# Six of eleven gate/up pairs of a feed-forward layer formed with seven block products in place of eight

## The chip, the cores and the metric

The kernel runs on one core of a Trainium2 chip. Its engines work side by side, each through its own queue in program order: TensorE (PE; PEld are its weight loads), VectorE (DVE), ScalarE (ACT), GpSimd (POOL) and SyncE (SP), which issues most of the transfers. The metric is the device time of one execution in microseconds (us).

## The reference, cut to what matters

One decoder layer over 256 tokens of width 2048, all in 32-bit floats: RMSNorm, two token mixers (gated linear attention and dilated attention) merged by gates, then the feed-forward part, which the change touches:

```
hf = _rmsnorm(x, ffn_norm[l])
gu = hf @ w_ffn_in[l]                       # 256 x 2048 times 2048 x 11264
gate, up = gu[..., :D_FF], gu[..., D_FF:]   # D_FF = 5632
x = x + (jax.nn.silu(gate) * up) @ w_ffn_out[l]
out = _rmsnorm(x, final_norm)
```

## The kernel before, in words

Every large product is a `Job`: a weight matrix's 512 columns, all of its rows, and two groups of 128 tokens (a "T" job). A job goes through its rows in k tiles of 128. One transfer (a unit, `raw`, three buffers) brings four k tiles of 512 columns, and a unit is worked off in two subs of two k tiles each. `split` writes a sub's weights as a rounded part `wh` (ScalarE, L121) and the rest `wl = raw - wh` (VectorE, L184), 1024 elements in each partition; there are `LA + 1 = 5` buffers of each. `mains` then issues three matmuls with 512 columns for each k tile and token group, hi·wh, hi·wl and lo·wh, where hi and lo are the two parts of the transposed activations: 12 matmuls in a sub, 96 in a job of 16 k tiles.

The order is written out by hand in the main loop at the end of the kernel. At each sub it calls `next_split` (the split of the sub four places on, and after a unit's last one the next transfer), then the evacuation of the job that has just ended (`pending.evac`), then a hook of the job, then `advance`, `mains` and `advance` again. `advance` takes a step of a queue of small tasks, such as `turn_block`, which transposes a finished block on TensorE into `psa` and splits it into hi and lo. So on ScalarE and VectorE the split of the sub four places on stands ahead of the evacuation of the job that has ended, and its `wh` buffer is the one that this job's last sub reads.

The feed-forward part has eleven pairs. `pair(p)` is a gate job (its evacuation is a Silu on ScalarE into `sg`) and an up job (its evacuation is two scalar_tensor_tensor on VectorE, L794, which multiply and push `turn_block`). After pairs 4 and 8, and at the end, `down` adds four jobs of `w_ffn_out`, over four, four and three pairs. PSUM has eight banks: `acc` is four, handed out in turn, `psa` is two and `psb` two. `fpair` takes the banks of successive jobs in turn, two `acc`, two `psb`, two `acc`, so that a job begins in banks that the job ahead of it did not use. The last job is issued by code of its own behind the loop.

## Time and profile before

| | |
|---|---|
| median of 3 runs | 1886.39 us (1885.41 to 1886.59) |
| the profiled execution's own time | 1885.85 us |
| its span, first to last instruction | 1884.1 us |
| TensorE busy | 1869.7 us, 99% of the span |
| VectorE busy | 1025.3 us, 54% |
| ScalarE busy | 861.5 us, 46% |
| granted TensorE clock, mean | 0.998 |

The profile gives each engine's busy time, the chain of work that ended last, and, for any stretch, the instructions in order with what ended the idle time before each. A matmul's row shows 0.39 us, but successive matmuls overlap, so the pace is read from the distance of their starts. An idle time of an engine other than TensorE costs nothing here as long as TensorE goes on.

### The profile page before, as it was taken

The page shows a single profiled execution, that of the slowest core. Times are in us where ns is not written, and L with a number is a line of the kernel's source. Part 1 is how long each engine was busy: PE and PEld are TensorE (multiplying, and loading weights), DVE is VectorE, ACT ScalarE, POOL GpSimd, SP SyncE. Part 2 cuts the span into 40 slices and gives each one's busy share as a digit, 9 for nine tenths or more (in the row PEclk, how much of TensorE's full clock was granted, in tenths as well). Part 3 has the DMA queues.
Part 4 walks back from the last instruction along what each step waited for, and adds up shares of the span by engine and source line. Part 5 has one row for each costly group of instructions (what it writes and reads, how often), then busy time and mean ns, then how long its engine had stood idle before and what let it go on. Part 6 is the DMA issues. An engine that isn't in the chain of part 4 may idle for free.

```text
span 1884.1 us, 22852 instructions
## 1 busy us (share of the span) xinstructions
PE 1869.7 (99%) x9324; PEld 1587.7 (84%) x9324; DVE 1025.3 (54%) x1146; ACT 861.5 (46%) x1071; POOL 22.3 (1%) x35
## 2 busy tenths in 40 slices
PE   8999999999999999999999999999999999999998
PEld 8988988888888888888888888888888888888886
DVE  6446646745665466555554555444455454454454
ACT  6446545544454454544444455444443444434443
POOL 0000000000000000000000000000000000000001
PEclk9999999999999999999999999999999999999999
DMA  7554455456555565465657655555555555555553
GB/s 251 205 198 158 167 189 165 162 184 195 174 174 179 200 193 172 161 218 199 207 190 243 231 179 195 186 199 180 198 181 200 193 187 184 196 189 191 196 182 114
DMA packets 207297, 356.31 MB, mean 189 GB/s; under 512 B 6123, under 2 KB 66599, under 8 KB 207192
## 3 DMA queue, kind: packets, MB, share of 16 engines
q1 hardware_dynamic: 202192, 346.18, 54.2%
q0 software_dynamic: 1728, 5.51, 1.3%
q10 hardware_dynamic: 3272, 3.16, 0.6%
q8 instruction: 73, 1.20, 0.3%
q14 instruction: 32, 0.26, 0.0%
HBM read 352.70 MB, written 2.13 MB: 188 GB/s over the span
## 4 chain that ended last, share of the span: by engine, by line
PE 98%; DVE 1%; ACT 0%; DMA 0%; issue 0%; SPq 0%; DVEq 0%; ACTq 0%
PE acc L234 67%; PE psb L234 12%; PE acc L216 9%; PE acc L218 5%; PE psa L696 1%; PE psa L550 0%; PE psb L595 0%; PE psa L471 0%; PE psb L453 0%; PE psb L560 0%; PE psb L597 0%; PE psa L571 0%; DMA o<-in_x_dram 0%; PE psa L301 0%; PE psa L234 0%; PE psb L398 0%
## 5 line engine op out<-in xcount | busy, mean ns | idle before, releaser
L184 DVE TENSOR_TENSOR wl<-raw,wh 128x1024 fp32r<-128x1024 f32 (+2 forms) x655 | 794.5, 1216 | 794.2 <-ACT wh L121 791.9
L121 ACT ACTIVATE wh<-raw 128x1024 fp32r<-128x1024 f32 (+2 forms) x655 | 685.5, 1049 | 874.2 <-PE acc L234 639.9
L234 PE MATMUL acc<-wh,h 128*128 128x512 f32 (+2 forms) x2496 | 768.5, 386 | 0.0
L234 PEld LDWEIGHTS acc<-wh,h 128*128 128x128 f32 x2496 | 467.2, 188 | 91.4 <-issue 2.0
L234 PE MATMUL acc<-wl,h 128*128 128x512 f32 (+2 forms) x1248 | 479.9, 385 | 0.0
L216 PE MATMUL acc<-h,wh 128*128 128x512 f32 x768 | 274.4, 401 | 0.0
L234 PEld LDWEIGHTS acc<-wl,h 128*128 128x128 f32 x1248 | 235.0, 188 | 44.2
L218 PE MATMUL acc<-h,wl 128*128 128x256 f32 x768 | 214.5, 279 | 0.0
L234 PE MATMUL acc<-wh,z 128*128 128x512 f32 (+1 forms) x648 | 199.2, 386 | 0.0
L216 PEld LDWEIGHTS acc<-h,wh 128*128 128x128 f32 x768 | 144.2, 188 | 34.4 <-ACT wh L121 0.7
L218 PEld LDWEIGHTS acc<-h,wl 128*128 128x128 f32 x768 | 144.8, 189 | 0.4
L234 PEld LDWEIGHTS acc<-wh,z 128*128 128x128 f32 x648 | 121.1, 188 | 24.3
L234 PE MATMUL acc<-wl,z 128*128 128x512 f32 (+1 forms) x324 | 125.0, 386 | 0.0
L234 PE MATMUL psb<-wh,h 128*128 128x512 f32 x384 | 119.9, 390 | 0.0
L234 PE MATMUL psb<-wh,z 128*128 128x512 f32 x304 | 94.9, 390 | 0.0
L234 PE MATMUL acc<-h,wh 128*128 128x256 f32 x512 | 92.5, 283 | 0.0
L234 PEld LDWEIGHTS psb<-wh,h 128*128 128x128 f32 x384 | 72.1, 188 | 14.9
L234 PEld LDWEIGHTS acc<-h,wh 128*128 128x128 f32 x512 | 80.0, 192 | 0.2
L234 PE MATMUL acc<-wh,o 128*128 128x512 f32 x256 | 79.5, 389 | 0.0
L234 PE MATMUL psb<-wl,h 128*128 128x512 f32 x192 | 74.7, 389 | 0.0
L234 PE MATMUL acc<-h,wl 128*128 128x256 f32 x256 | 72.4, 283 | 0.0
L234 PEld LDWEIGHTS acc<-wl,z 128*128 128x128 f32 x324 | 60.9, 188 | 12.1
(202 smaller groups left out, 1151.9 us busy)
## 6 DMA issues: line engine op xcount, KB each, us to landing
raw<-in_w_in_dram SPq DMA_DIRECT2D x144, 1024.0 KB, 4.7
raw<-in_w_ffn_in_dram SPq DMA_DIRECT2D x88, 1024.0 KB, 4.8
raw<-in_w_ffn_out_dram SPq DMA_DIRECT2D x44, 1024.0 KB, 5.0
raw<-in_w_branch_gla_dram SPq DMA_DIRECT2D x16, 1024.0 KB, 5.0
raw<-in_w_out_dram SPq DMA_DIRECT2D x16, 1024.0 KB, 5.0
...
```

What stands on the lines that cost most here:

```text
L121: nc.scalar.activation(o, i, func, **kw)
L184: nc.vector.tensor_sub(wl[:, :k * n], src, wh[:, :k * n].bitcast(F32))
L216: nc.tensor.matmul(job.acc[j], wh[:, kk, j * P:(j + 1) * P], hl.both(aj), start=first, stop=last, skip_group_check=True)
L218: nc.tensor.matmul(job.acc[j][:, 0:S], wl[:, kk, j * P:(j + 1) * P], hi, start=False, stop=last, skip_group_check=True)
L234: nc.tensor.matmul(dst, st, mv, start=first and i == 0 and j % per_bank == 0, stop=last and i == 2, skip_group_check=True)
L696: nc.tensor.transpose(pt[:, j * S + a * P:j * S + a * P + P], src[:, a, j * P:(j + 1) * P], ident)
```

## The change

Pairs 1, 3, 4, 6, 8 and 10 become one job of kind "S" each, which forms gate and up together. A unit of it is one step: two k tiles, with the 512 columns of gate and the 512 of up, brought by two transfers. In steps 0, 1, 2, 4, 5 and 6 of eight (`FAST`) the block product of two token groups by two k tiles with two k tiles by gate and up is formed by Strassen's algorithm in Winograd's form: seven block products in place of eight, so 21 matmuls in place of 24. They take sums of weight blocks (`sums`, three subtractions on VectorE into `t`) and sums of activation blocks (`x1_forms`, made once after the norm, six steps). Steps 3 and 7 keep eight products. A fast step has four subs with 3, 6, 6 and 6 matmuls (`b11`, `b2`, `t13`, `t24`); a plain step two with 12.

The products of a job stand in all eight PSUM banks; `evac_step1` and `evac_step2` add them up into gate and up. The other five pairs stay two "T" jobs, but now always with `acc` for gate and `psb` for up. `turn_up` holds the transposition of a T pair that stands ahead of an S job until the S job has ended. `down` now follows pairs 3 and 7, and `fpair` counts the down jobs alone. `final_norm` is loaded at the last `down`.

```diff
+            if st in job.fast:
+                plan = (("b11", ((0, "a11", "p1"),)), ("b2", ((0, "a12", "p2"), (1, "s4", "p3"))),
+                        ("t13", ((0, "s1", "p5"), (1, "s3", "p7"))), ("t24", ((0, "s2", "p6"), (1, "a22", "p4"))))
...
+    def sums(sub):
...
+        if sub["src"] == "t13":
+            t = sub["unit"]["t"] = env["fp"].tile([P, 4, 512], F32, name="t", tag="t")
+            nc.vector.tensor_sub(t[:, 0:2], b[:, :, 1], b[:, 0])
+        else:
+            t = sub["unit"]["t"]
+            nc.vector.tensor_sub(t[:, 2], b[:, 1, 1], t[:, 0])
+            nc.vector.tensor_sub(t[:, 3], b[:, 1, 0], t[:, 2])
...
+    def step_mains(sub):
...
+            acc = [ps_acc() for _ in range(4)] + ps_pair(2) + ps_pair(3)
+            job.bank = dict(zip(("p1", "p2", "p3", "p5", "p7", "p6", "p4", "p8"), acc))
...
+            act(wh, src, AF.Copy)
+            nc.vector.tensor_sub(wl, src, wh.bitcast(F32))
...
+    FAST = (0, 1, 2, 4, 5, 6)
...
+    def x1_forms():
...
+            nc.vector.tensor_add(a, t[:, :, 0].bitcast(F32), t[:, :, 1].bitcast(F32))
+            nc.vector.tensor_add(f[:, 0], a[:, 0, P:], a[:, 1, P:])
+            nc.vector.tensor_sub(f[:, 2], a[:, 0, 0:P], a[:, 0, P:])
+            nc.vector.tensor_sub(f[:, 1], f[:, 0], a[:, 0, 0:P])
+            nc.vector.tensor_sub(f[:, 3], a[:, 1, 0:P], f[:, 1])
...
+            act(b[:, 0], f, AF.Copy)
+            nc.vector.tensor_sub(b[:, 1], f, b[:, 0].bitcast(F32))
...
+    def evac_step1(job):
...
+        act(u[0], b["p1"], AF.Copy)
+        nc.vector.tensor_add(u[1], u[0], b["p6"])
+        nc.vector.tensor_add(u[2], u[1], b["p7"])
+        nc.vector.tensor_add(u[1], u[1], b["p5"])
+        nc.vector.tensor_add(u[3], u[2], b["p5"])
...
+    def evac_step2(p):
...
+            nc.vector.tensor_add(z[:, 0], u[0], b["p2"])
+            act(z[:, 0], z[:, 0], AF.Silu, scale=env["rstd2"][:, 0:1])
...
-    def pair(p):
-        for col, ev in ((512 * p, evac_fgate(p)), (FF + 512 * p, evac_fup(p))):
+    def pair(p, hold):
+        for col, ev in ((512 * p, evac_fgate(p)), (FF + 512 * p, evac_fup(p, hold))):
...
-                    {5: lambda: drain("X")} if first else None, pairs=fpair()))
+                    {5: lambda: drain("X")} if first else None, pairs=[3] if col >= FF else [0]))
+
+    def fast_pair(p):
+        def start():
+            drain("F")
+            drain("A")
+            drain("A2")
...
+        job.pre[len(job.subs) - 2] = lambda: evac_step1(job)
...
-            pre = {2 * (n - 1): lambda: drain("A")} if c == 0 else None
+            pre = {2 * (n - 2): lambda: drain("A"), 2 * (n - 1): lambda: drain("A2")} if c == 0 else None
...
+    fastp = (1, 3, 4, 6, 8, 10)
     for p in range(11):
-        pair(p)
-        if p == 4:
-            down(0, 4, False)
-        if p == 8:
-            down(4, 4, False)
+        if p in fastp:
+            fast_pair(p)
+        else:
+            pair(p, p + 1 in fastp and p != 7)
+        if p in (3, 7):
+            down(p - 3, 4, False)
...
+            if i + 1 < len(subs):
+                sums(subs[i + 1])
             split(subs[i])
```

On VectorE, the end of the up job of pair 1 and the first subs behind it before (`wl` is a split's second half, `raw` the weights as they were loaded, `sg` the pair's block in evacuation):

```order
L184 TENSOR_TENSOR wl_9800<-raw_9696,wh_9799 128x1024 [waits Activation_49]
L184 TENSOR_TENSOR wl_9818<-raw_9735,wh_9817 128x1024 [waits DMAHW5_49,Activation_49]
L184 TENSOR_TENSOR wl_9834<-raw_9735,wh_9833 128x1024 [waits Activation_49]
L184 TENSOR_TENSOR wl_9852<-raw_9769,wh_9851 128x1024 [waits DMAHW6_49,Activation_49]
L794 SCALAR_TENSOR_TENSOR sg_9714<-acc_9717,r_ffn_9306,sg_9714 128x512
L794 SCALAR_TENSOR_TENSOR sg_9714<-acc_9718,r_ffn_9306,sg_9714 128x512 [waits PE_49]
L184 TENSOR_TENSOR wl_9874<-raw_9769,wh_9873 128x1024 [waits Activation_49]
```

and one fast step of the first S job now (`t` holds the sums of weight blocks):

```order
L275 TENSOR_TENSOR wl_9737<-raw_9663,wh_9736 128x512 [waits DMAHW4_49,Activation_49]
L194 TENSOR_TENSOR t_9746<-raw_9663 128x1024 [waits DMAHW5_49,DVE_49]
L275 TENSOR_TENSOR wl_9749<-raw_9663,wh_9748 128x1024 [waits Activation_49]
L197 TENSOR_TENSOR t_9746<-raw_9663,t_9746 128x512 [waits DVE_49]
L198 TENSOR_TENSOR t_9746<-raw_9663,t_9746 128x512 [waits DVE_49]
L275 TENSOR_TENSOR wl_9761<-t_9746,wh_9760 128x1024 [waits Activation_49]
L275 TENSOR_TENSOR wl_9777<-t_9746,wh_9776 128x1024 [waits Activation_49]
```

For the weights of two k tiles with gate and up, VectorE had two instructions over 1024 elements and has seven, four over 1024 and three over 512.

On TensorE, the first six matmuls of a gate job before (its two banks are the two `acc`):

```order
L234 MATMUL acc_12195<-wh_12119,h0_8791 128x512 [waits Activation_49]
L234 MATMUL acc_12195<-wl_12120,h0_8791 128x512 [waits DVE_49]
L234 MATMUL acc_12195<-wh_12119,h0_8791 128x512
L234 MATMUL acc_12196<-wh_12119,h0_8791 128x512
L234 MATMUL acc_12196<-wl_12120,h0_8791 128x512
L234 MATMUL acc_12196<-wh_12119,h0_8791 128x512
```

and of the gate job behind the first S job now (`acc_9980` and `acc_9981` are the banks that held the products p1 and p2):

```order
L339 MATMUL acc_9980<-wh_9900,h0_8787 128x512 [waits Activation_49]
L339 MATMUL acc_9980<-wl_9901,h0_8787 128x512 [waits DVE_49]
L339 MATMUL acc_9980<-wh_9900,h0_8787 128x512
L339 MATMUL acc_9981<-wh_9900,h0_8787 128x512 [waits DVE_49]
L339 MATMUL acc_9981<-wl_9901,h0_8787 128x512
L339 MATMUL acc_9981<-wh_9900,h0_8787 128x512
```

The fourth matmul has a wait on VectorE that it had not. On VectorE, what stands at that border now, from the S job's last split to the first add that reads p2 (`u` and `sg` are what the products are added into):

```order
L275 TENSOR_TENSOR wl_9889<-raw_9780,wh_9888 128x1024 [waits DMAHW3_49,Activation_49]
L286 TENSOR_TENSOR wl_9901<-raw_9830,wh_9900 128x1024 [waits DMAHW4_49,Activation_49]
L286 TENSOR_TENSOR wl_9911<-raw_9830,wh_9910 128x1024 [waits Activation_49]
L286 TENSOR_TENSOR wl_9923<-raw_9873,wh_9922 128x1024 [waits DMAHW5_49,Activation_49]
L943 TENSOR_TENSOR u1_9927<-u0_9926,psa_9629 128x512 [waits Activation_49]
L944 TENSOR_TENSOR u2_9928<-u1_9927,psa_9629 128x512 [waits DVE_49]
L945 TENSOR_TENSOR u1_9927<-u1_9927,acc_9628 128x512 [waits DVE_49]
L946 TENSOR_TENSOR u3_9929<-u2_9928,acc_9628 128x512
L286 TENSOR_TENSOR wl_9948<-raw_9873,wh_9947 128x1024 [waits Activation_49]
L286 TENSOR_TENSOR wl_9966<-raw_9892,wh_9965 128x1024 [waits DMAHW6_49,Activation_49]
L952 TENSOR_TENSOR sg_9969<-u0_9926,acc_9626 128x512
```

Five splits of the next job and four adds stand between the S job's last split and the add that frees p2's bank. The next job has the bank at once, where the job behind an evacuation had other banks before.

On VectorE in the up job of pair 0, where `x1_forms` runs now (`fa` and `ff` are its scratch, `o1` its result; before, the two `wl` followed each other):

```order
L286 TENSOR_TENSOR wl_9368<-raw_9220,wh_9367 128x1024 [waits Activation_49]
L871 TENSOR_TENSOR fa_9373<-h1_8788 128x512
L872 TENSOR_TENSOR ff_9374<-fa_9373 128x128 [waits DVE_49]
L873 TENSOR_TENSOR ff_9374<-fa_9373 128x128
L874 TENSOR_TENSOR ff_9374<-ff_9374,fa_9373 128x128 [waits DVE_49]
L875 TENSOR_TENSOR ff_9374<-fa_9373,ff_9374 128x128 [waits DVE_49]
L879 TENSOR_TENSOR o1_9380<-ff_9374,o1_9380 128x512 [waits Activation_49]
L286 TENSOR_TENSOR wl_9396<-raw_9262,wh_9395 128x1024 [waits DMAHW1_49,Activation_49]
```

Six such groups stand between successive splits, behind those of pair 0's first to sixth up sub. On ScalarE the copy that L879 waits for stands between the `wh` of the two splits.

## Rows read from the trace of the kernel before

**Rows 1.** The page: busy us, share of the span; then shares of the chain.
```profile
PE 1869.7 (99%) x9324; PEld 1587.7 (84%) x9324; DVE 1025.3 (54%) x1146; ACT 861.5 (46%) x1071; POOL 22.3 (1%) x35
...
PE 98%; DVE 1%; ACT 0%; DMA 0%; issue 0%; SPq 0%; DVEq 0%; ACTq 0%
```

**Rows 2.** Timeline of TensorE, up job of pair 0: start us, duration us, instruction, count.
```profile
1168.02 0.39 PE L234 MATMUL psb<-wh,h 128*128 128x512 f32 x1
...
1189.78 0.39 PE L234 MATMUL acc<-wh,h 128*128 128x512 f32 x1
```

**Rows 3.** Timeline of VectorE in pairs 0 and 1, idle time before in brackets.
```profile
1191.08 1.23 DVE L184 TENSOR_TENSOR wl<-raw,wh 128x1024 fp32r<-128x1024 f32 x1 [1.50 <-ACT wh L121]
1192.22 1.40 DVE L794 SCALAR_TENSOR_TENSOR sg<-psb,r_ffn,sg 128x512 f32<-128x512 f32 x2
```

**Rows 4.** Timeline of VectorE where its instructions follow each other closely.
```profile
456.69 2.36 DVE L184 TENSOR_TENSOR wl<-raw,wh 128x1024 fp32r<-128x1024 f32 x2 [0.33 <-PE psa L571]
458.97 0.75 DVE L319 TENSOR_TENSOR z<-acc,fold 128x256 f32<-128x256 f32 x2
459.75 0.69 DVE L321 TENSOR_TENSOR z<-z,R 128x512 f32<-128x512 f32 x1
460.36 0.55 DVE L577 TENSOR_TENSOR l<-psa,e 128x384 fp32r<-128x384 f32 x1
...
464.03 0.68 DVE L590 TENSOR_TENSOR vl<-z,vh 128x128 fp32r<-128x128 f32 x3
```

**Rows 5.** Groups of ScalarE and VectorE, feed-forward stretch 1151 to 1875 us: busy, mean ns.
```profile
L184 DVE TENSOR_TENSOR wl<-raw,wh 128x1024 fp32r<-128x1024 f32 x258 | 317.5, 1232 | 350.9 <-ACT wh L121 350.9
...
L121 ACT ACTIVATE wh<-raw 128x1024 fp32r<-128x1024 f32 x257 | 272.6, 1061 | 399.2 <-PE acc L234 264.8 <-PE psb L234 134.2
L121 ACT ACTIVATE z<-psa 128x512 fp32r<-128x512 f32 x22 | 11.8, 587 | 0.0
```

**Rows 6.** Timeline of all engines where up job 4 ends and a down job begins.
```profile
1367.44 0.39 PE L234 MATMUL psb<-wh,z 128*128 128x512 f32 x1
...
1367.63 1.06 ACT L121 ACTIVATE wh<-raw 128x1024 fp32r<-128x1024 f32 x1 [1.66 <-PE acc L234]
...
1368.73 1.23 DVE L184 TENSOR_TENSOR wl<-raw,wh 128x1024 fp32r<-128x1024 f32 x1 [1.50 <-ACT wh L121]
...
1369.87 1.40 DVE L794 SCALAR_TENSOR_TENSOR sg<-acc,r_ffn,sg 128x512 f32<-128x512 f32 x2
```

**Rows 7.** The same view some us later: a finished block is transposed and split.
```profile
1372.88 1.03 PE L696 MATMUL psa<-ident,sg 128*128 128x128 f32 x8
...
1373.67 0.48 PE L234 MATMUL psb<-wh,z 128*128 128x512 f32 x1
...
1374.04 1.07 ACT L121 ACTIVATE z<-psa 128x512 fp32r<-128x512 f32 x2
...
1375.31 1.28 DVE L105 TENSOR_TENSOR z<-psa,z 128x512 fp32r<-128x512 f32 x2
```

**Rows 8.** Timeline of TensorE at the kernel's start, matmuls of 348 columns.
```profile
6.65 1.08 PE L301 MATMUL psb<-ident,o 128*128 128x128 f32 x4 [1.57 <-DMA o<-in_x_dram]
...
8.46 0.49 PE L234 MATMUL acc<-wh,h 128*128 128x348 f32 x1
8.75 0.49 PE L234 MATMUL acc<-wl,h 128*128 128x348 f32 x1
...
10.78 0.40 PE L234 MATMUL acc<-wh,h 128*128 128x348 f32 x1
...
12.05 0.32 PE L234 MATMUL acc<-wl,h 128*128 128x348 f32 x1
12.21 0.48 PE L234 MATMUL acc<-wh,h 128*128 128x348 f32 x2
```

**Rows 9.** Stretches at the end: length, busy us of the engines, granted clock (PEclk), DMA.
```profile
1875.50:1878.00 2.50, 0.05 (x1) 0.00 (x0) 1.17 (x6) 0.91 (x4) 0.00 (x0) 1.00 0.00 0
1878.00:1884.00 6.00, 0.00 (x0) 0.00 (x0) 1.59 (x4) 0.72 (x1) 0.00 (x0) 0.50 0.46 175
```

More of the change, by code (lines that the diff above doesn't have):

```diff
@@ L145, in trunk_layer, with add_steps @@
     nc.vector.memset(epst, EPS)
+    def add_steps(job):
+        seen = {}
+        for st in range(job.nkt // 2):
+            unit = dict(job=job, k0=2 * st, k=2, raw=None)
+            units.append(unit)
+            if st in job.fast:
+                plan = (("b11", ((0, "a11", "p1"),)), ("b2", ((0, "a12", "p2"), (1, "s4", "p3"))),
+                        ("t13", ((0, "s1", "p5"), (1, "s3", "p7"))), ("t24", ((0, "s2", "p6"), (1, "a22", "p4"))))
+            else:
+                plan = tuple((f"b{a + 1}", ((0, f"a1{a + 1}", "p2"), (1, f"a1{a + 1}", "p3"),
+                                            (0, f"a2{a + 1}", "p4"), (1, f"a2{a + 1}", "p8"))) for a in range(2))
+            for src, prods in plan:
+                sub = dict(job=job, unit=unit, step=st, src=src, idx=len(job.subs), prods=[])
+                for f, a, b in prods:
+                    pr = dict(f=f, a=a, b=b, first=b not in seen, last=False)
+                    seen[b] = pr
+                    sub["prods"].append(pr)
+                job.subs.append(sub)
+                subs.append(sub)
+        for pr in seen.values():
+            pr["last"] = True
+        for i, s in enumerate(job.subs):
+            s["last"] = i == len(job.subs) - 1
@@ new lines, in raw_step @@
+    def raw_step(unit):
+        return unit["raw"].rearrange("p (a c n) -> p a c n", a=2, c=2)
+    def sums(sub):
+        if sub.get("src") not in ("t13", "t24"):
+            return
+        b = raw_step(sub["unit"])
+        if sub["src"] == "t13":
[5 more added lines that the diff above has]
+            nc.vector.tensor_sub(t[:, 3], b[:, 1, 0], t[:, 2])
@@ new lines, in step_src, with step_acts @@
+    def step_src(sub):
+        b = raw_step(sub["unit"])
+        src = sub["src"]
+        if src == "b11":
+            return b[:, 0, 0:1]
+        if src[0] == "b":
+            return b[:, int(src[1]) - 1]
+        return sub["unit"]["t"][:, 0:2] if src == "t13" else sub["unit"]["t"][:, 2:4]
+    def step_acts(job, st, a):
+        if a[0] == "s":
+            f = job.forms(st)
+            return [f[:, w, int(a[1]) - 1] for w in range(2)]
+        hl, j = job.acts(2 * st + int(a[2]) - 1)
+        q = slice(0, P) if a[1] == "1" else slice(P, 2 * P)
+        return hl.hi(j)[:, q], hl.lo(j)[:, q]
@@ new lines, in step_mains @@
+    def step_mains(sub):
+        job = sub["job"]
+        if not hasattr(job, "bank"):
+            acc = [ps_acc() for _ in range(4)] + ps_pair(2) + ps_pair(3)
+            job.bank = dict(zip(("p1", "p2", "p3", "p5", "p7", "p6", "p4", "p8"), acc))
+        for pr in sub["prods"]:
+            wh, wl = (t[:, pr["f"]] for t in sub["w"])
+            hi, lo = step_acts(job, sub["step"], pr["a"])
+            for i, (st, mv) in enumerate(((hi, wh), (hi, wl), (lo, wh))):
+                nc.tensor.matmul(job.bank[pr["b"]], st, mv, start=pr["first"] and i == 0,
+                                 stop=pr["last"] and i == 2, skip_group_check=True)
@@ L150, in add @@
         job.units = []
+        if job.kind == "S":
+            add_steps(job)
+            return
         u1 = 0
@@ L171, in dma @@
         r0 = job.row0 + unit["k0"] * P
+        if job.kind == "S":
+            for a in range(2):
+                w = job.w[r0 + a * P:r0 + a * P + P]
+                nc.sync.dma_start(raw_step(unit)[:, a],
+                                  bass.AP(tensor=w.tensor, offset=w.offset + job.col0,
+                                          ap=[list(w.ap[0]), [job.col1 - job.col0, 2], [1, n]]))
+            return
         nc.sync.dma_start(unit["raw"][:, :k * n].rearrange("p (a n) -> p a n", a=k),
@@ L188, in mains @@
         job = sub["job"]
+        if job.kind == "S":
+            step_mains(sub)
+            return
         n = job.ncols
@@ L763, in ffn_norm_chunk @@
             env["rstd2"] = col_rstd("ffn", tot, D)
+            push("F", x1_forms())
     def evac_out(c):
@@ L788, in evac_fgate, with turn_up, evac_fup @@
         return go
-    def evac_fup(p):
+    held = []
+    def turn_up(p, z, hold):
+        aT[p] = hl_block("z", 2 * p % 8)
+        held.append(turn_block(z, aT[p]))
+        if not hold:
+            while held:
+                push("A" if len(held) > 1 else "A2", held.pop(0))
+    def evac_fup(p, hold):
         def go(job):
```

53 lines of the change are left out of this document (46 added, 7 removed).

## The prediction

> **What bounds the kernel now.** I read the page first: TensorE is busy for 1869.7 of 1884.1 us and carries 98% of the chain of work that ended last; VectorE has 1025.3 us of work and ScalarE 861.5 [rows 1]. Then I read the pace of the part that changes. The up job of pair 0 starts at 1168.02 and the next job at 1189.78 [rows 2]: 21.76 us for 96 matmuls of 512 columns, 0.2267 us each, 2.72 us for a sub of twelve. VectorE subtracts once in each sub: 1.23 us, after 1.5 us idle until ScalarE's next `wh` [rows 3], and that `wh` waits for TensorE to give back its buffer; VectorE idles 350.9 us for it in the whole part [rows 5]. So TensorE sets the pace, and VectorE has a lead of four subs and no more, since there are five buffers.
>
> Because VectorE's work grows, its packed pace matters, not its durations. Two subtractions over 1024 elements take 2.36 us together, so the second starts 1.14 us after the first [rows 4]. A 512-element one is followed 0.61 us after its start (459.75 to 460.36); one that needs the result of the one just ahead starts 0.03 us after that one's end (458.97 + 0.75 to 459.75), so 0.72 us after its start. Three over 128 elements take 0.68 us, 0.20 apart [rows 4].
>
> **The change part by part.**
>
> *Matmuls.* 6 pairs x 6 steps x 3 products of parts = 108 fewer: 108 x 0.2267 = 24.5 us of TensorE time. A pair needs 43.5 us as two T jobs; an S job, with 6 x 21 + 2 x 24 = 174 matmuls, needs 39.4.
>
> *A fast step.* TensorE needs 21 x 0.2267 = 4.76 us. VectorE has four instructions over 1024 elements and three over 512, one of these waiting for its neighbour: 4 x 1.14 + 2 x 0.61 + 0.72 = 6.5 us. The last split needs ScalarE's copy of the last sum, 1.06 us [rows 5] plus a hand-over at each end, and finds one split of 1.14 to cover it: I add 0.1, so 6.6 us. ScalarE's own part, 3.5 x 1.06 = 3.7 us, fits. So VectorE sets the pace of the fast steps. Before, the same two k tiles had 2 x 1.14 us on VectorE against 5.44 on TensorE.
>
> *An S job.* At its start the splits of its first step are done. VectorE then has: the wait for the buffer and a 512-element `wh`, 0.65; that sub's split, 0.61; the evacuation of the job ahead, 1.32 (two instructions take 1.40, of which the next one overlaps 0.08 [rows 3]); the rest of step 1, 6.0; steps 2, 4, 5 and 6, 26.4; the two plain splits of step 3, 2.3. That is 37.3 us until the last split of step 6. TensorE then has, after about 0.2 us for the result to land, 5 matmuls of that sub (1.1 us) and the plain step 7 (5.44): 44.0 us. The plain steps give back what they can in this sum, as VectorE never waits in it. Against 43.5 us for the pair: +0.5 us, six times: **+3.0**. The saved matmuls are spent on waiting for VectorE.
>
> *The border behind an S job.* The next job gets the banks of p1 and p2. p1's is free early; p2's by the add that stands, on VectorE, behind the split of that job's fifth sub. From the last split of step 6 VectorE has two plain splits and three of the next job (5 x 1.14), the four adds of `evac_step1` (0.60 + 2 x 0.72 + 0.60), two more splits (2.3), and the add (0.69): 11.3 us. TensorE has in that time 0.2 + 1.1 + 5.44, and three matmuls into p1's bank, 0.7: 7.4 us. It stands still for 3.9 us, six times: **+23.4**. Without any lateness of VectorE the lower bound is read from a border of the kernel before: next job at 1367.44, `wh` at 1367.63, `wl` at 1368.73, evacuation from 1369.87 [rows 6], so 2.43 us plus 0.69 less 0.7, or 2.4 us. I take 3.9, since the count of instructions gives it.
>
> *Pair 7 into `down`.* The first down job behind up job 7 gets the same two `psb` banks. By the same rows its first matmul waits 2.43 + 0.74 = 3.2 us: **+3.2**. Borders of the kernel before have no such wait, as the banks alternate.
>
> *The last `down`.* Two finished blocks are now turned in its first job, each drained right ahead of the sub that reads it. In the rows of such a task, the transpositions start at 1372.88 and the next matmul could at 1373.67, but the first half-block's lo part is there only at 1375.31 + 0.68 [rows 7]; the third matmul, due at 1374.1, would wait 1.9 us. Twice: **+3.8**, between 0 (if the tasks are through earlier) and that. Before, only one block was pending, with two subs to spare.
>
> *The activation sums.* Each of the six groups stands between two splits, and both engines wait for each other: split 1.14, the five short ones 0.72 + 0.20 + 0.20 + 0.31 + 0.28 = 1.7, ScalarE's copy 0.59 [rows 5], then its next `wh` 1.06, with hand-overs 4.55 us for a sub that TensorE does in 2.72. After six, 11.0 us late. A split is done 2.5 us after the start of the sub four ahead (1367.44 to 1369.96 [rows 6]), so the lead is 10.9 - 2.5 = 8.4. TensorE waits 2.6 us, and VectorE enters the first S job 1.8 us late: **+4.4**, at least 0.
>
> *At nothing:* bytes loaded are the same, in 512 KB transfers, whose unit now lasts 6.6 us in place of 5.4; an S unit's transfer is due two steps later. The later load of `final_norm` has one down job (16 us) ahead of its use. Eleven transposed blocks stay eleven. TensorE's work of the next subs covers each; were weights late, every S step could wait, but the chain has 0% DMA [rows 1].
>
> **The sum.** +3.0 + 23.4 + 3.2 + 3.8 + 4.4 = +37.8 us on the profiled execution's 1885.85: 1923.7. The median is 0.5 us above that execution, so **1924 us**, 2.0% slower.
>
> Bounds. Low: borders at 2.4 (-9), no cost at the last `down` and the sums (-8), S jobs at 43.2 (-5): 1902. High: if VectorE's instructions did not overlap (1.23 and 0.69 us in full), a step takes 7.0 us, a job 2.1 more and a border 0.9 more, 18 us in all: 1942. The Trainium skill, "VectorE: DVE Perf Modes", section Terms, has it so: a flush after every instruction keeps the next from starting until the pipe is empty. By that the time would be 1942; the rows, where the next starts 0.08 us ahead of the end, are against it.
>
> **The rivals.**
>
> *The clock falls.* TensorE never stood still for long in this trace. At the end, its last matmul ended at about 1875.6 and the granted clock was 1.0 until 1878.0 and 0.5 (1.2 GHz) after that [rows 9], 2.5 us later. At the start, matmuls of 348 columns came 0.29 us apart, and 0.16 apart by 12.05; TensorE had worked without a break from 6.65, and the last matmul at the slow pace is that of 10.78, whose row is the first short one [rows 8]. So a border wait of 3.9 us can cost the clock, and each fall up to 4.3 us at half pace, 2.1 us: seven times, 15 us, 1939, which is inside my range. Worse if the short gaps of the fast steps (1.8 us of every 6.6, in pieces) do it: a step would need 21 x 0.45 = 9.5 us of TensorE, up to 2.9 more in 36 steps, up to 104 us: 2028. It decides by whether the clock stays at 1.0 within the S jobs. For it: the fall at the end. Against it: the gaps are short. Chance of this worse case 0.11.
> The Trainium skill has a rule for it ("TensorE: Matmul & The Clock Gate", "A second HAM failure mode: psum-queue depth-cycling"): frequent small idle times between groups of matmuls were seen to make the clock swing between its two levels. By that rule this rival would hold; no run here shows it.
>
> *VectorE does not hold TensorE up.* If the three- and four-dimensional patterns of the sums and splits ran faster than the flat rows, by a third or more, a step would need at most 4.76 us, the S jobs 39.4, and the borders only the 2.4: -24.5 + 14.7 + 3.2 + 3.8 = -2.8 us, 1883, no change. At twice the pace the split ahead of the evacuation halves too, the borders cost 1.5, and it ends at 1876, faster. The point is 4.76 us for seven instructions. For it: over the whole part VectorE has work for half of the time only (317.5 us of splits in 724 [rows 5]), so its total would fit. Against it: every two-operand row, in SBUF or PSUM, shows the same pace: from 0.61 us for 512 elements to 1.14 for 1024, 1.04 ns an element [rows 4]. Chances 0.05 (no change) and 0.03 (faster).
>
> **How the numbers follow.** The forecast's case has 0.81, the clock's worse case 0.11, the other two 0.08. The range, 1900 to 1955, takes in the low bound, the high bound and a clock that falls at borders on top of part of it; the worse case and the two on the other side lie outside. 0.2% is 3.8 us, about what a measurement of this kernel can tell from no change. Faster by more 0.03, within it 0.05, slower by more 0.92.
>
> **What would show it.** In the profile after, VectorE's idle time in the S jobs should be almost nil and a fast step should last 6.6 us, with TensorE waiting for `wl` (L275). S jobs of 44 us against 43.5 confirm the pace; 39.4 refute it. The matmul into p2's bank should wait for the add at L952 for 3.9 us in six places, the down job behind pair 7 for L933, 3.2 us. The L879 group should make TensorE wait in pair 0's up job. A granted clock of 0.5 inside S jobs would mean the first rival. I would be wrong at the root if VectorE shows long idle times inside the fast steps.

## The result, and the profile after

The changed kernel takes 1917.95 us (median of 4 runs, 1917.54 to 1918.85) against 1886.46 of the kernel before on the same chip: a ratio of 1.0169 (95% interval 1.0157 to 1.0182). It is 31.5 us slower; 1924 us had been forecast, 1900 to 1955 as the range. TensorE works 108 matmuls less, and the kernel is longer all the same. The page of the changed kernel, lines that answer to [rows 1]:

```profile
PE 1866.2 (97%) x9216; PEld 1566.6 (82%) x9216; DVE 1211.6 (63%) x1410; ACT 919.0 (48%) x1155; POOL 22.3 (1%) x35
...
PE 81%; DVE 11%; issue 3%; ACT 3%; DMA 1%; ACTq 0%; DVEq 0%; SPq 0%
```

The share of the chain is the line to read: VectorE had 1% of it and has 11%, although it is busy for 63% of the span only. The profiled execution (1917.97 us) comes to the feed-forward part at the same place as before (up job 0 starts at 1168.00 against 1168.02 in [rows 2]); TensorE's last matmul ends 32.1 us later. So all of the loss lies in the part that was changed, and the starts of the jobs on TensorE divide it. In the lines of the changed kernel L227 is a matmul of an S job and L339 one of any other job; L275 and L286 are VectorE's splits of the same two kinds, L194, L197 and L198 the sums of weight blocks; L132 is ScalarE (`wh`, a block's hi part, a Silu), L801 the transposing of a block and L116 its lo part; L933 is the evacuation of a T pair, L943 to L946 the adds of `evac_step1`, L952 to L959 `evac_step2`. An edit that adds or takes out a line above them moves these numbers by one.

| term of the prediction | forecast | measured, us |
|---|---|---|
| six S jobs, against 43.5 for a pair | +3.0 | +6.3 (44.5 to 44.6 each; the first 46.2, of which 1.6 stand in the next row) |
| activation sums | +4.4 | +4.1 (2.5 in up job 0, 1.6 in the first S job) |
| borders behind five S jobs | +19.5 | +7.3 (1.07, 0.97, 2.21, 1.02, 2.06) |
| pair 7 into `down` | +3.2 | +5.0 (3.3, and 1.7 by the clock) |
| last `down`, its border included | +7.7 | +9.5 |
| sum | +37.8 | +32.2 |

**The fast step.** TensorE in the second and third step of the first S job:

```profile
1198.86 0.50 PE L227 MATMUL acc<-wl,h 128*128 128x512 f32 x1 [0.79 <-DVE wl L275]
...
1201.32 0.49 PE L227 MATMUL acc<-wl,o 128*128 128x512 f32 x1 [0.81 <-DVE wl L275]
...
1205.49 0.50 PE L227 MATMUL acc<-wl,h 128*128 128x512 f32 x1 [0.46 <-DVE wl L275]
...
1207.95 0.50 PE L227 MATMUL acc<-wl,o 128*128 128x512 f32 x1 [0.79 <-DVE wl L275]
```

and VectorE beside it, one step from its first to its last instruction (the last row is two splits):

```profile
1202.48 0.69 DVE L275 TENSOR_TENSOR wl<-raw,wh 128x512 fp32r<-128x512 f32 x1
1203.08 1.22 DVE L194 TENSOR_TENSOR t<-raw 128x1024 f32<-128x1024 f32 x1
1204.21 1.22 DVE L275 TENSOR_TENSOR wl<-raw,wh 128x1024 fp32r<-128x1024 f32 x1
1205.35 0.69 DVE L197 TENSOR_TENSOR t<-raw,t 128x512 f32<-128x512 f32 x1
1206.07 0.69 DVE L198 TENSOR_TENSOR t<-raw,t 128x512 f32<-128x512 f32 x1
1206.68 2.51 DVE L275 TENSOR_TENSOR wl<-t,wh 128x1024 fp32r<-128x1024 f32 x2
```

The wait for the same `wl` comes back after 6.63 us (1198.86 to 1205.49, 1201.32 to 1207.95). No VectorE row here has an idle time in brackets, where the split in [rows 3] had 1.50 ahead of it. The starts follow each other by 0.60, 1.13, 1.14, 0.72 and 0.61, as in [rows 4]. The groups of 1194 to 1238 us show it in sum, as [rows 5] did for the kernel before (busy, mean ns, idle time before):

```profile
L275 DVE TENSOR_TENSOR wl<-t,wh 128x1024 fp32r<-128x1024 f32 x11 | 13.4, 1222 | 0.7 <-ACT wh L132 0.3
...
L194 DVE TENSOR_TENSOR t<-raw 128x1024 f32<-128x1024 f32 x5 | 6.1, 1219 | 0.0
...
L198 DVE TENSOR_TENSOR t<-raw,t 128x512 f32<-128x512 f32 x5 | 3.5, 692 | 0.2
```

**The border behind an S job.** VectorE and then TensorE behind the first one:

```profile
1233.83 3.49 DVE L286 TENSOR_TENSOR wl<-raw,wh 128x1024 fp32r<-128x1024 f32 x3
1237.24 0.68 DVE L943 TENSOR_TENSOR u<-u,psa 128x512 f32<-128x512 f32 x1
...
1239.28 0.68 DVE L946 TENSOR_TENSOR u<-u,acc 128x512 f32<-128x512 f32 x1
1239.88 2.35 DVE L286 TENSOR_TENSOR wl<-raw,wh 128x1024 fp32r<-128x1024 f32 x2
1242.15 0.68 DVE L952 TENSOR_TENSOR sg<-u,acc 128x512 f32<-128x512 f32 x1
```

```profile
1240.02 0.50 PE L339 MATMUL acc<-wh,h 128*128 128x512 f32 x1 [0.75 <-DVE u L946]
```

VectorE's order is the one of the forecast, and its add for p2 (L952) ends at 1242.83. The fourth matmul does not wait for it; it starts at 1240.02, behind L946, the last add that reads p5. An idle time of 0.75 costs 1.0 to 1.1 us (1.07 by the starts of the jobs): the row after the one that waited starts 0.33 later and not 0.23, and an idle time is counted from the end of the matmul ahead, 0.39 after its start.

Behind two of the borders (pairs 5 and 9) the next job also transposes the S job's block, and that waits for the evacuation's last instructions, here at pair 5; this is the other 1.1 us of the 2.21 and 2.06:

```profile
1470.75 0.33 PE L801 MATMUL psa<-ident,sg 128*128 128x128 f32 x1 [0.43 <-DVE sg L959]
1471.42 0.98 PE L801 MATMUL psa<-ident,sg 128*128 128x128 f32 x7 [0.34 <-DVE sg L959]
```

**Pair 7 into `down`, and the last `down`.** TensorE's waits there:

```profile
1604.59 0.76 PE L339 MATMUL psb<-wh,z 128*128 128x512 f32 x1 [3.16 <-DVE sg L933]
...
1839.59 0.50 PE L339 MATMUL acc<-wh,z 128*128 128x512 f32 x1 [2.31 <-ACT z L132]
...
1841.26 1.22 PE L339 MATMUL acc<-wh,z 128*128 128x512 f32 x2 [0.88 <-DVE z L116]
...
1850.86 0.50 PE L339 MATMUL acc<-wh,z 128*128 128x512 f32 x1 [0.81 <-ACT z L132]
...
1852.23 0.73 PE L339 MATMUL acc<-wh,z 128*128 128x512 f32 x2 [0.64 <-DVE z L116]
```

The first wait of the last `down` (2.31) has a late transfer in it. ScalarE and VectorE behind the last S job, ahead of its second evacuation:

```profile
1832.29 1.06 ACT L132 ACTIVATE wh<-raw 128x1024 fp32r<-128x1024 f32 x1 [3.97 <-DMA raw<-in_w_ffn_out_dram]
...
1833.38 1.23 DVE L286 TENSOR_TENSOR wl<-raw,wh 128x1024 fp32r<-128x1024 f32 x1 [0.99 <-ACT wh L132]
```

ScalarE's copy waits for its weights, and VectorE stands idle for 0.99 us ahead of L952, so that the block is finished that much later. In three other runs with the same idle time (0.95 to 1.02 us, in e2_more_sums, e4_banks and e5_no_forms) the first wait is 2.27 to 2.37 us; in e10_p5_late (below), where the border moves VectorE and TensorE alike and VectorE has no such idle time, it is 1.25. About 1.0 of the 2.31 is therefore the weights'. Behind the other S jobs ScalarE waits for weights too (1.8 to 3.1 us), but VectorE at most 0.12 for it; in e3_fast4 ScalarE has no such wait.

Stretches of the changed kernel in the columns of [rows 9]: length, busy us of PE, PEld, DVE, ACT and POOL, granted clock, DMA share, GB/s. The first is the first S job, the others lie around these waits:

```profile
1194.00:1239.00 45.00, 40.60 (x170) 30.93 (x169) 44.13 (x48) 25.50 (x28) 0.00 (x0) 1.00 0.55 194
...
1604.60:1608.00 3.40, 3.40 (x8) 2.72 (x9) 0.50 (x1) 0.00 (x0) 0.00 (x0) 0.50 0.25 98
...
1840.10:1846.90 6.80, 5.92 (x14) 4.51 (x14) 1.70 (x3) 0.91 (x1) 0.00 (x0) 0.50 0.48 154
```

In the S job VectorE is busy for 44.13 of 45.00 us and the clock is 1.00. Behind the two long waits it is 0.50, which is 1.2 GHz: 8 and 14 matmuls 0.43 us apart and not 0.23, so 1.7 and 2.8 us.

### The profile page after: what moved, and what is told of

It reads as the page before. It is cut to its first block, busy times and chain, and to the rows that moved or that the text cites. A ratio compares the mean times of both kernels' runs of the same rounds, so it can differ in the third digit from the quotient of the medians.

```text
span 1916.3 us, 23191 instructions
## 1 busy us (share of the span) xinstructions
PE 1866.2 (97%) x9216; PEld 1566.6 (82%) x9216; DVE 1211.6 (63%) x1410; ACT 919.0 (48%) x1155; POOL 22.3 (1%) x35
## 3 DMA queue, kind: packets, MB, share of 16 engines
q10 hardware_dynamic: 3272, 3.16, 0.6%
## 4 chain that ended last, share of the span: by engine, by line
PE 81%; DVE 11%; issue 3%; ACT 3%; DMA 1%; ACTq 0%; DVEq 0%; SPq 0%
PE acc L339 53%; PE acc L321 9%; PE psb L339 9%; PE acc L323 5%; DVE wl L275 4%; ACT wh L132 3%; DVE t L194 2%; DVE wl L286 2%; DVE t L198 1%; DVE t L197 1%; PE psa L801 1%; PE psa L655 0%; PE psb L700 0%; PE psa L576 0%; PE psb L558 0%
## 5 line engine op out<-in xcount | busy, mean ns | idle before, releaser
L286 DVE TENSOR_TENSOR wl<-raw,wh 128x1024 fp32r<-128x1024 f32 (+2 forms) x559 | 674.7, 1214 | 605.6 <-ACT wh L132 603.5
L132 ACT ACTIVATE wh<-raw 128x1024 fp32r<-128x1024 f32 (+3 forms) x655 | 662.2, 1023 | 697.6 <-PE acc L339 492.9
L339 PE MATMUL acc<-wh,h 128*128 128x512 f32 (+2 forms) x1792 | 552.4, 385 | 2.8 <-DVE u L946 2.8
L339 PEld LDWEIGHTS acc<-wh,h 128*128 128x128 f32 x1792 | 334.9, 188 | 68.5 <-DVE u L946 4.5
L339 PE MATMUL acc<-wl,h 128*128 128x512 f32 (+2 forms) x896 | 342.9, 383 | 0.0
L339 PE MATMUL acc<-wh,z 128*128 128x512 f32 (+1 forms) x712 | 222.7, 391 | 6.0 <-ACT z L132 3.1
L323 PE MATMUL acc<-h,wl 128*128 128x256 f32 x768 | 214.5, 279 | 0.0
L339 PEld LDWEIGHTS acc<-wl,h 128*128 128x128 f32 x896 | 168.9, 189 | 30.4 <-DVE wl L286 0.2
L339 PEld LDWEIGHTS acc<-wh,z 128*128 128x128 f32 x712 | 134.3, 190 | 35.3 <-ACT z L132 3.6
L339 PE MATMUL acc<-wl,z 128*128 128x512 f32 (+1 forms) x356 | 138.5, 389 | 0.0
L132 ACT ACTIVATE wh<-t 128x1024 fp32r<-128x1024 f32 x72 | 76.4, 1061 | 117.6 <-DVE t L194 57.1
L275 DVE TENSOR_TENSOR wl<-raw,wh 128x512 fp32r<-128x512 f32 (+1 forms) x96 | 96.5, 1021 | 17.2 <-ACT wh L132 17.2
L339 PE MATMUL psb<-wh,h 128*128 128x512 f32 x320 | 99.7, 389 | 0.5 <-ACT wh L132 0.5
L275 DVE TENSOR_TENSOR wl<-t,wh 128x1024 fp32r<-128x1024 f32 x72 | 88.0, 1222 | 11.0 <-ACT wh L132 8.9
L339 PE MATMUL acc<-h,wh 128*128 128x256 f32 x512 | 92.5, 283 | 0.0
L227 PE MATMUL acc<-wh,h 128*128 128x512 f32 x240 | 83.8, 390 | 0.0
L339 PEld LDWEIGHTS acc<-h,wh 128*128 128x128 f32 x512 | 80.0, 192 | 0.2
L339 PE MATMUL acc<-wh,o 128*128 128x512 f32 x256 | 79.4, 389 | 0.0
L339 PE MATMUL psb<-wh,z 128*128 128x512 f32 x240 | 76.1, 395 | 3.2 <-DVE sg L933 3.2
```

What stands on the lines that cost most here:

```text
L132: nc.scalar.activation(o, i, func, **kw)
L227: nc.tensor.matmul(job.bank[pr["b"]], st, mv, start=pr["first"] and i == 0, stop=pr["last"] and i == 2, skip_group_check=True)
L275: nc.vector.tensor_sub(wl, src, wh.bitcast(F32))
L286: nc.vector.tensor_sub(wl[:, :k * n], src, wh[:, :k * n].bitcast(F32))
L323: nc.tensor.matmul(job.acc[j][:, 0:S], wl[:, kk, j * P:(j + 1) * P], hi, start=False, stop=last, skip_group_check=True)
L339: nc.tensor.matmul(dst, st, mv, start=first and i == 0 and j % per_bank == 0, stop=last and i == 2, skip_group_check=True)
```

## The experiments

Each is compared with the kernel before on the same chip (the ratio) and, in us, with the 1917.95 of the changed kernel. Diffs are against the changed kernel where nothing else is said.

**Is it VectorE's pace? The sums taken out and doubled.** The two runs move the same work in both directions.

```diff
-        if sub.get("src") not in ("t13", "t24"):
-            return
+        return
...
-        return sub["unit"]["t"][:, 0:2] if src == "t13" else sub["unit"]["t"][:, 2:4]
+        return b[:, 0] if src == "t13" else b[:, 1]
```

> Leaves out VectorE's sums of weight blocks: the subs t13 and t24 split weights as they were loaded, so the output is not the reference's; the matmuls stay. Theory (VectorE's seven instructions set the pace of a fast step): 3 x 1.14 + 0.61 = 4.0 us of VectorE are left for a step, under TensorE's 4.76, so the S jobs go from 44.5 to 39.4 us, the first one loses its late start, the waits of 0.8 us for wl inside the steps go, and the border waits shrink: about 1880 us, 1875 to 1887. Rival (the S jobs are slow for another reason: two transfers in a unit, ScalarE's copies, the change of banks after every three matmuls): stays at 1918.

e1_no_sums: 1882.03 us (ratio 0.9977, 0.9965 to 0.9989). Five of the S jobs take 39.44 us each, which is 174 matmuls at 0.2267 (the other, behind the first `down`, 40.46). The border's wait for the same add (L945 in this run) becomes shorter and does not go: 0.11 to 0.46 us at the six borders.

```diff
             nc.vector.tensor_sub(t[:, 0:2], b[:, :, 1], b[:, 0])
+            nc.vector.tensor_sub(t[:, 2:4], b[:, :, 1], b[:, 0])
```

> One more subtraction over 1024 elements on VectorE in each fast step, whose result is written over. Theory: a step gets 1.14 us longer, five of the six steps of a job show it in full and the first is done ahead: S jobs 50 to 51 us, 34 to 41 us in all, 1952 to 1959. Rival (another cause holds the S jobs, VectorE has room): 1918 to 1922.

e2_more_sums: 1953.74 us (1.0356, 1.0336 to 1.0377), with S jobs of 50.1 to 50.3; the first, with 6.8 us at the lower clock in it, took 52.96. Taking the sums out gives 35.9 us, and TensorE is then the bound; one more per step takes 35.8. TensorE's matmuls are the same in all three, so VectorE's instructions in the fast steps set the pace of the changed kernel.

**What do the activation sums cost?**

```diff
-            f = job.forms(st)
-            return [f[:, w, int(a[1]) - 1] for w in range(2)]
+            hl, j = job.acts(2 * st + int(a[1]) % 2)
+            return hl.hi(j)[:, 0:P], hl.lo(j)[:, 0:P]
...
-            push("F", x1_forms())
```

> Leaves out the sums of activation blocks (x1_forms): the products that take them read a block as it is, so the output is not the reference's. Theory: pair 0's up job loses its wait of 2.5 us and the first S job its late start of 1.6: 1914, and the first S job is as long as the others, 44.6 us. Rival (the late start comes from the S job's own beginning, not from the groups): the up job alone gets shorter, 1915.5, and the first S job stays at 46.2.

e5_no_forms: 1913.09 us (1.0142, 1.0125 to 1.0159), 4.9 less; up job 0 takes 21.76 and the first S job 44.63, so 2.5 and 1.6 are theirs. The other 0.8 fits a stretch at the lower clock in the last `down` that lasted 3.4 us in this run and 6.8 in the changed kernel.

**Whose bank does the border wait for?** Each run issues one add four times, the first that of p5 (L946), the second that of p2 (L952).

```diff
-        nc.vector.tensor_add(u[3], u[2], b["p5"])
+        for _ in range(4):
+            nc.vector.tensor_add(u[3], u[2], b["p5"])
```

> The changed kernel with the add into u[3] (L946, the last instruction that reads p5) issued four times in place of once; it gives the same values each time. Theory from the trace: the job behind an S job has the bank of p5, not of p2, as its second one, so the wait at its fourth matmul grows by three adds, 3 x 0.7 = 2.1 us, at each of six borders: 0.7 becomes 2.8 us, +13 us, 1931 (1928 to 1935; plus up to 1.7 a place if the clock falls behind such a wait). Rival (the prediction's bank): the job waits for p2's add, which only moves by the 2.1 us that VectorE is later, and had about 1 us to spare: +1 a border, 1924.

e10_p5_late: 1932.4 us (1.0245, 1.0225 to 1.0266; two runs, 1929.67 and 1935.13, the second one profiled). The add and the fourth matmul behind the second S job (the inserted line makes L946 to L947), and the stretch behind it:

```profile
1333.26 2.84 DVE L947 TENSOR_TENSOR u<-u,acc 128x512 f32<-128x512 f32 x4
```

```profile
1336.16 0.50 PE L339 MATMUL acc<-wh,z 128*128 128x512 f32 x1 [2.81 <-DVE u L947]
```

```profile
1337.00:1340.30 3.30, 3.30 (x9) 2.61 (x8) 3.30 (x6) 0.82 (x2) 0.00 (x0) 0.50 0.47 149
```

All six waits grew to 2.81 to 2.92. At the second to the fifth of them the clock fell; behind the first, of 2.92, and the sixth, of 2.84, it did not.

```diff
-            nc.vector.tensor_add(z[:, 0], u[0], b["p2"])
+            for _ in range(4):
+                nc.vector.tensor_add(z[:, 0], u[0], b["p2"])
```

> The changed kernel with the add that frees p2's bank (L952) issued four times in place of once; it gives the same values each time. It is the counterpart of e10_p5_late. Theory: no matmul of the job behind an S job waits for p2's bank, so the 2.1 us that this puts into VectorE's queue at each of six borders show only where the block's transposing waits for the evacuation (two gate jobs and perhaps the last down): 1918 to 1925, likeliest 1921. Rival (the prediction's bank): the job waits for it, +2.1 us at each of six borders, 1931 or more with the clock's falls.

e9_p2_late: 1927.88 us (1.022, 1.0199 to 1.024), 3 us above what was expected of the theory. The fourth matmul behind the first S job, the transposing behind the third, and the last `down`:

```profile
1241.10 0.50 PE L339 MATMUL acc<-wh,h 128*128 128x512 f32 x1 [0.77 <-DVE u L946]
...
1475.32 0.33 PE L801 MATMUL psa<-ident,sg 128*128 128x128 f32 x1 [2.88 <-DVE sg L960]
...
1850.66 0.80 PE L339 MATMUL acc<-wh,z 128*128 128x512 f32 x1 [4.62 <-ACT z L132]
```

All six border waits are 0.65 to 0.77, behind L946, as they were: p2's bank is not what the next job waits for. The time went where the block is transposed: 0.43 to 2.88 and, behind the fifth S job, to 2.39, each with 3.4 us at the lower clock that had not been counted (4.0 and 3.7 us together with it), and 2.31 to 4.62 in the last `down`.

**The wait behind pair 7.** The `down` jobs behind it start in `acc` banks:

```diff
         if p in (3, 7):
+            if p == 7:
+                turn[0] = 2
             down(p - 3, 4, False)
```

> The first down job behind pair 7 takes two acc banks, not the psb banks of up job 7 (one line sets the turn). Theory: the wait of 3.2 us for the evacuation at L933 goes, and with it the fall of the clock right behind it (3.4 us at the lower level, 1.7 us lost): 1913.0. Rival (the clock falls there for another reason, such as the S job ahead): 3.3 us only, 1914.7, with a stretch at the lower clock near 1605 us.

e4_banks: 1911.48 us (1.0132, 1.0117 to 1.0147), 6.5 less. The same border on TensorE, and its stretch:

```profile
1600.79 0.39 PE L339 MATMUL psb<-wh,h 128*128 128x512 f32 x1
1601.02 0.39 PE L339 MATMUL acc<-wh,z 128*128 128x512 f32 x1
```

```profile
1595.00:1608.00 13.00, 13.00 (x63) 10.87 (x62) 6.85 (x8) 5.58 (x6) 0.00 (x0) 1.00 0.54 167
```

The wait is gone and so is the fall of the clock: 3.3 + 1.7. The rest, 1.5, fits the last `down`, where the clock was low for 3.4 us and not 6.8.

**The last `down`.** The blocks of pairs 9 and 10 are transposed earlier. The recorded expectation says one and two subs; on TensorE each comes one sub earlier (12 and 36 matmuls of the last `down` stand ahead of them, where 24 and 48 did):

```diff
-    def turn_block(src, hl):
+    def turn_block(src, hl, wait=3):
...
-        held.append(turn_block(z, aT[p]))
+        held.append(turn_block(z, aT[p], {9: 1, 10: 2}.get(p, 3)))
```

> The changed kernel, but the finished blocks of pairs 9 and 10 are transposed one and two subs earlier, ahead of the point at which the last down drains them. Theory: the first job of the last down lost 2.31 + 0.88 + 0.81 + 0.64 us to waits for the transposed blocks' hi and lo parts and about 3.4 us to the clock at half for 6.8 us behind the first of them; with the blocks ready both go: 1918 - 8 = 1910 us (1908 to 1913). Rival: the clock falls there anyway, for another reason than the wait: 1913 to 1915, with a 0.5 stretch in the last down.

e6_early_turn: 1913.3 us (1.0145, 1.013 to 1.016): 4.7 less, and the 8 were too many. What is left of the four waits, and the clock of the stretch:

```profile
1839.78 0.50 PE L339 MATMUL acc<-wh,z 128*128 128x512 f32 x1 [1.27 <-ACT z L132]
...
1841.26 0.73 PE L339 MATMUL acc<-wh,z 128*128 128x512 f32 x2 [0.74 <-DVE z L116]
```

```profile
1825.00:1905.00 80.00, 74.94 (x368) 62.22 (x366) 48.84 (x61) 37.59 (x57) 8.78 (x8) 1.00 0.48 164
```

Two waits of 2.0 in sum are left of 4.6, since the first block's parts still queue behind the S job's evacuation, and VectorE waits 0.88 us in it for the late weights here too; the clock no longer falls there, so the rival is out. From the first matmul of the last `down` to the end it is 5.9 us; this run came to the feed-forward part 1.3 us later.

**Which rate of fast steps can VectorE follow?**

```diff
-    FAST = (0, 1, 2, 4, 5, 6)
+    FAST = (0, 2, 4, 6)
```

> The changed kernel with every second step of an S job fast (0, 2, 4 and 6) in place of six of eight. Theory: VectorE sets the pace of a fast step (6.6 us against 4.76 of TensorE) and has 2.3 us for a plain one (against 5.44). In turns, VectorE needs 4 x 6.6 + 4 x 2.3 = 35.6 us in a job and TensorE 4 x 4.76 + 4 x 5.44 = 40.8, so TensorE sets the pace again: S jobs of 40.8 us (44.5 in the changed kernel, 43.5 for the pair before), with VectorE idle for 5 us in each. As VectorE is then not late at a job's end, the 0.65 to 0.77 us wait for L946 at the borders goes or becomes shorter, and the activation sums, four groups now, cost under 1 us in place of 4.1. What has nothing to do with it stays: 3.2 us (and perhaps 1.7 for the clock) at pair 7 into down, 8 us in the last down, up to 1 us twice where a gate job waits for the transposed block. From the kernel before: -6 x 2.7 + 3.2 to 5 + 8 + 2 + 0 to 1 = about 1884 us (1880 to 1888), ratio 0.999. Rival: the interleaving of seven short instructions per step, not VectorE's total, holds TensorE up; then the S jobs stay at 43 or more and the time is 1900 or more.

e3_fast4: 1884.23 us (0.9992, 0.9982 to 1.0001). The first S job on all engines:

```profile
1190.30:1231.10 40.80, 40.80 (x182) 33.78 (x181) 37.03 (x40) 24.25 (x25) 0.00 (x0) 1.00 0.67 226
```

TensorE is busy for all of its 40.80 us, VectorE for 37.03; the border wait for L946 is gone. A third of the saved matmuls given back, and the kernel is 33.7 us shorter than with all of them.

With the two other repairs (`turn[0] = 2` and the earlier transposing):

> Every second step fast as in e3_fast4, the down jobs behind pair 7 in the acc banks as in e4_banks, and the finished blocks of pairs 9 and 10 transposed one and two subs earlier. Theory: the three losses are independent of each other, so that this run is e3_fast4 less 3.2 to 5 us (the banks behind pair 7) and less 5 to 8 us (the waits and the clock fall in the first job of the last down): 1872 to 1878 us, ratio 0.993 to 0.996, faster than both kernels; the granted clock stays at 1.0 from the first S job to the last matmul. Rival: waits of the last down only move to other places (the early transposing waits for evacuation results), and the time is within 2 us of e3_fast4.

e7_all: 1876.66 us (0.995, 0.9935 to 0.9965), 7.6 less than e3_fast4. That is within what was expected, though less than the 6.5 and 4.7 that the two repairs gave alone. Part of the difference is a wait in a new place: on TensorE, the S job behind pair 3's `down` waits at its seventh matmul for the evacuation of the last `down` job, and now the one behind pair 7's `down` does so too.

```profile
1408.70 0.50 PE L227 MATMUL acc<-wh,o 128*128 128x512 f32 x1 [1.70 <-DVE o L968]
```

So the `down` jobs were put into banks that the S job needs late: in `pairs` 0 and 1 are two `acc` banks and 3 is `psb`, so that the last job of a `down` ahead of an S job ends in `psb` (this diff is against e7_all):

```diff
-            add(Job("T", w_ffn_out, p0 * 512, 4 * n, 512 * c, 512, 4, acts, evac_down(c, last), pre, pairs=fpair()))
+            add(Job("T", w_ffn_out, p0 * 512, 4 * n, 512 * c, 512, 4, acts, evac_down(c, last), pre, pairs=[(0, 3, 0, 1 if last else 3)[c]]))
...
-            if p == 7:
-                turn[0] = 2
```

> e7_all with the four down jobs behind pairs 3 and 7 in acc, psb, acc, psb, so that the last of them ends in psb. In e7_all the S job behind such a group of down jobs waited twice for 1.70 us at its seventh matmul for L968, the evacuation of that last down job, and took 42.8 in place of 40.8 us. Theory: the seventh matmul opens p3's bank, the third acc bank that the S job takes, and with the last down job in psb, which the S job needs only in its third and fourth sub, the wait goes: all six S jobs 40.8 us, -4.0 us, 1872.7 us (1871.5 to 1874), ratio 0.993. Rival: the wait moves to p4 or p8 in psb and comes back there in part: 1874.5 to 1876.7.

e11_banks2: 1872.58 us (0.9929, 0.9912 to 0.9945), all S jobs 40.80: it is faster than both kernels. Its page:

```profile
PE 1854.8 (99%) x9252; PEld 1574.8 (84%) x9252; DVE 1158.0 (62%) x1338; ACT 904.7 (48%) x1129; POOL 22.3 (1%) x35
...
PE 97%; DVE 1%; ACT 1%; issue 0%; DMA 0%; SPq 0%; DVEq 0%; ACTq 0%
```

Against the kernel that it is built on, `FAST = (0, 1, 3, 4, 6)`:

> e11_banks2 with five fast steps (0, 1, 3, 4 and 6) in place of four. TensorE needs 5 x 4.76 + 3 x 5.44 = 40.1 us in an S job, VectorE 5 x 6.6 + 3 x 2.3 = 39.9: each pair of fast steps costs VectorE 3.7 us of its lead and each plain step gives 3.2 back. Theory: the lead of four subs covers that, S jobs of 40.1 to 40.6, one more activation group (+0.8 in the up job of pair 0), the borders' wait for L947 back in part (0 to 0.5): -4.1 + 0.8 + 0 to 3 + 0 to 3: between 3 us faster and 3 us slower than e11_banks2, 1870 to 1876; likeliest 1871.5. Rival: VectorE's packing loses more than the sums say, so that S jobs take 42 or more: 1880 or more.

e12_fast5: 1878.28 us (0.9958, 0.9943 to 0.9973), 2 us beyond the upper end. S jobs took 41.5 to 41.6. The sum of 39.9 for VectorE had left out the evacuation of the job ahead, which the prediction's own sum for an S job had: 5 x 6.63 + 3 x 2.28 + 1.32 = 41.3, over TensorE's 40.1. VectorE at the beginning of the second S job, where that evacuation (L934) stands between two splits; for the next 25 us it has no idle time:

```profile
1278.88 0.69 DVE L275 TENSOR_TENSOR wl<-raw,wh 128x512 fp32r<-128x512 f32 x1 [1.07 <-ACT wh L132]
1279.49 1.40 DVE L934 SCALAR_TENSOR_TENSOR sg<-psb,r_ffn,sg 128x512 f32<-128x512 f32 x2
1280.81 1.22 DVE L194 TENSOR_TENSOR t<-raw 128x1024 f32<-128x1024 f32 x1
```

**Can GpSimd take part of it?**

```diff
-            nc.vector.tensor_sub(t[:, 2], b[:, 1, 1], t[:, 0])
-            nc.vector.tensor_sub(t[:, 3], b[:, 1, 0], t[:, 2])
+            nc.gpsimd.tensor_sub(t[:, 2], b[:, 1, 1], t[:, 0])
+            nc.gpsimd.tensor_sub(t[:, 3], b[:, 1, 0], t[:, 2])
```

> The changed kernel with the two chained 512-element subtractions of each fast step (t[:, 2] and t[:, 3]) on GpSimd in place of VectorE. VectorE is left with 5.3 us a step by its own rows. GpSimd's instructions over 512 elements take 1.29 us each (L972), 2.6 us a step. In the last down of the changed kernel VectorE's split beside one of them took 1.97 us in place of 1.23. Theory: the two slow each other, so that 2.6 us of GpSimd cost VectorE about 2.1 us: a step of 7.4 us in place of 6.6, S jobs of 49, +28 us, 1946 (1925 to 1965). Rival: no such cost: a step of 5.3 us, S jobs of 40.5 to 41.5, 1897 (1892 to 1903).

e8_pool: 1978.15 us (1.0486, 1.0465 to 1.0507), beyond the upper end. VectorE and GpSimd in the second S job:

```profile
1328.33 1.22 DVE L275 TENSOR_TENSOR wl<-raw,wh 128x1024 fp32r<-128x1024 f32 x1
1329.62 2.15 DVE L275 TENSOR_TENSOR wl<-t,wh 128x1024 fp32r<-128x1024 f32 x1
...
1334.04 1.23 DVE L275 TENSOR_TENSOR wl<-t,wh 128x1024 fp32r<-128x1024 f32 x1 [2.27 <-ACT wh L132]
...
1338.21 2.16 DVE L275 TENSOR_TENSOR wl<-t,wh 128x1024 fp32r<-128x1024 f32 x1
```

```profile
1328.55 2.14 POOL L197 TENSOR_TENSOR t<-raw,t 128x512 f32<-128x512 f32 x1 [4.22 <-issue]
1330.77 2.15 POOL L198 TENSOR_TENSOR t<-raw,t 128x512 f32<-128x512 f32 x1
```

A step takes 8.59 us (1329.62 to 1338.21). Side by side both are slower, 2.15 us against 1.22 and 2.14 against the 1.29 of GpSimd's multiplication over as many elements (L972), and the ends tell how. GpSimd's first sum ends at 1330.69; the split that started at 1329.62 ends 1.08 later, at 1331.77; GpSimd's second sum, started at 1330.77, ends 1.15 after that, at 1332.92. Each seems to do its work only when the other has ended. The Trainium skill, "SBUF — State Buffer", section Who interferes with whom, says that a VectorE instruction with two SBUF inputs contends with a GpSimd instruction that reads SBUF, over a port that only one of them can hold; these rows agree. The expectation had the slowing only; it missed that the last split now waits for two slow sums in a row and ScalarE's copy, 2.27 us.

## Why the prediction was right, and where not

**The pace: right.** A fast step was put at 6.6 us from the starts in [rows 4] and takes 6.63. The Trainium skill, "VectorE: DVE Perf Modes", section Terms, has each instruction wait for the pipe to empty; by that and the full durations the estimate would be 7.0. The row at 1204.21 starts 0.09 us ahead of the end of the one at 1203.08, so the rows differ from that section here as well. The S jobs came out 0.5 us longer than the 44.0 of the sum. The step is 0.2 of it, six times 0.03, and the start 0.26: the first split starts 0.91 us after the job (1285.71 against 1284.80 in the second S job), where 0.65 had been taken; the small rest is not assigned. As e1_no_sums and e2_more_sums changed the work of VectorE alone, this cause is shown.

**The border: wrong, and the largest error.** The mis-sized term is 3.9 us at six borders, for a wait for p2's bank. VectorE's part of its working holds: from the end of the last split of step 6 (1230.42 + 1.22) to the end of L952 (1242.83) are 11.2 us, where 11.3 had been counted. The step that failed is "the next job gets the banks of p1 and p2". The text ahead of the prediction says the same of `acc_9981`, and it is wrong there too: that bank held p5. In the code the reads of p1 and p5 end in `evac_step1`, those of p2 and p3 only in `evac_step2`, and the next job got the two that came free first, so the wait ends with L946, 2.9 us earlier. With 0.75 of idle time a border costs about 1.0 us, below even the 2.4 that the prediction had as its lower bound, since that bound had the wrong bank in it too. e10_p5_late and e9_p2_late show it from both sides: only p5's add moves the wait. That banks go out in the order in which they come free, and not in the one in which they were asked for, is read from these waits and the code. With it, VectorE's instructions in the section on the change would have told the answer: L946 stands three places ahead of L952 there.

**Pair 7 into `down`: right** (3.16 idle, 3.2 forecast), and e4_banks takes it away. The clock behind it is the prediction's first rival in its mild form, inside the range: 1.7 us.

**The last `down`: mechanism right, term too small.** 3.8 had been taken for two drains; four waits cost 4.6 us of idle time, and the clock 2.8. The first drain waits 2.31 and not 1.9, its hi and lo parts being queued on ScalarE and VectorE behind the S job's evacuation, and about 1.0 of that are the weights that came late. The prediction had put late weights at nothing, as TensorE's work of the next subs would cover them and the chain had 0% DMA; the chain now has 1%, and here the work did not cover them. e6_early_turn shows that the clock's part and more than half of the idle time hang on the place of the transposing.

**The activation sums: right** (4.1 against 4.4; e5_no_forms shows both places).

**The rivals.** The clock's worse case fell: in the S jobs it stays at 1.00 with two waits of 0.46 and 0.8 us in every 6.63. The rule of the Trainium skill that spoke for it ("TensorE: Matmul & The Clock Gate", "A second HAM failure mode: psum-queue depth-cycling") is therefore not borne out by this kernel. With more and longer waits it is in part: e2_more_sums has one stretch of 6.8 us at the lower clock in its first S job, behind a wait of 2.18 us, and e8_pool, with four waits of 2.6 us in sum in each step, has eight of 3.4 us in its six S jobs. That VectorE would not hold TensorE up fell with the idle times of 0.0 in its groups.

The forecast was 6 us too high, by errors in both directions: 12 us too much at the five borders, and 6 to 7 too little in the S jobs, the last `down` (its border included) and the clock. That it came so near owes something to this.
